# One decoder layer on one core: later w_ada loads, alternating half-array matmuls, and gathers, scores and gate loads in other places

## The chip, the cores and the metric

The kernel runs on one core of a Trainium2 chip. The time is what the device takes for one execution, in microseconds (us), and the value that counts is the median of the runs. A comparison of two such kernels can tell a difference of about 0.5% from no difference.

## What is computed

One decoder layer, 512 tokens of width 1024. Cut to what matters here:

```
mod = silu(c) @ w_ada + b_ada            # 6 vectors of 1024: sh1 sc1 gt1 sh2 sc2 gt2
h   = LN(x) * (1 + sc1) + sh1
z   = h @ w_in                           # q k v of two mixers, gates
ya  = differential attention, 8 heads, two softmax maps of key size 64 each, causal
ym  = chunkwise mLSTM, 4 heads, chunks of 128
y   = sigmoid(g_attn) * (ya @ w_br_attn) + sigmoid(g_ml) * (ym @ w_br_mlstm)
x   = LN_affine(ALPHA * x + gt1 * (y @ w_out))
h   = LN(x) * (1 + sc2) + sh2
q   = h @ peer_wq                        # 8 heads, two halves of 64 each
s   = q . sub_keys                       # 128 scores per half; top 16 of each,
                                         # then top 16 of their sums: 128 experts per token
out = sum over the 128 experts of softmax * gelu(h . u[e]) * v[e]
x   = LN_affine(ALPHA * x + gt2 * out)
```

## The kernel before

All matrix products run in split precision: an operand is a float16 high part and a float16 rest, and a product is three matmuls (high·high, high·rest, rest·high; `mm3_one`). The split costs one ScalarE and one VectorE instruction per piece (`split`, L168 and L169). Every weight piece is 128x1024 float32, goes through one of three `raw` buffers (L173) and ends in one of eight `w2` buffers.

The order of TensorE's instructions is the order in which the program is written: `Ordered` links each matmul to the one before. A scheduler places the instructions of the other engines and of the DMA queues; `P.before(r)` tells it to place r behind the last matmul written so far. That link is an order in the schedule and carries no semaphore. A queue works strictly in its order: SyncE issues nearly all loads, ScalarE the stores, GpSimd (POOL) the gathers, and an instruction that waits holds up those behind it. A `Filler` hands out TensorE work (a group of matmuls at a time) between the steps of attention, mLSTM and routing.

The stages, in us of the profiled span:

- To 84: layer norm, the first two w_ada vectors, the first projections.
- 84 to 330, attention. 32 steps of (head, query block): `at_s` (L436) computes two score maps m = 0 and 1. Map m takes rows 64m to 64m+63 of q and k, so each of its matmuls uses half of the array's rows: three matmuls of n columns (n = 128, 256, 384, 512 for the four query blocks) and one 128-row matmul that adds the causal mask (`negm`, `identb`). Before, map 0 is written whole, then map 1. Beside it `presplit` loads pieces of the tables q and u into `pre`, splits them and stores them to DRAM (`us`).
- 330 to 412, the mLSTM's last heads (`ml_s`, `ml_v`, `ml_y`; decay tiles `E`, L644 to L661).
- 412 to 570, the merge: 8 steps j, each with up to four groups of 24 matmuls. In each step `mod_col` (L306) is called for gt1, sc2, sh2 and gt2: it loads one 128x1024 block of w_ada into a `raw` buffer (tile `wad`, L311) and reduces it with one VectorE instruction (L312). These 32 blocks are the last 32 of 48. Nothing but a free buffer holds their loads back.
- 570 to 640: output projection, layer norm, h2. `gate_row` turns a column vector into a broadcast row with 8 transposes; the row h2r of token tile 0 is stored to DRAM (`h2d`).
- 640 to 1030, routing. `route(t)` for the token tiles t = 1 to 3 (t = 0 runs before): `scores` (L925) computes 4 heads of one half (12 matmuls of 64 rows), `top16` (L917 to L921) picks; then one-hot products build the dense gate matrix, staged in `gstage` and stored to DRAM (`gd`). TensorE's filler work here is the first 72 of 128 blocks of `u` (`u_pair`), whose results go to DRAM (`actd`). Tile 0 is done sparsely: `fetch` (L865) gathers a row of u per token, `dots` (L873) multiplies it with h2r. `some(dotg, n)` hands out dots: one after each of the four banks of a route, one in each of its nine one-hot steps.
- 1030 to 1060, change-over: buffers of the front part are released, h2r and gt2's row (`g2r`) are made ready, the first gate blocks (`gblk`, L1259) are loaded from `gd`.
- 1060 to 1465: `u_round(n)` and `v_round` alternate. A u round computes 4 blocks of u; a v round multiplies 4 blocks of gated activations with v: 4 times 18 matmuls. `some(sp, rate)` hands out gathers of tile 0: 7.2 in a u round, 4 in a v round (`SP_V` = 1.0 per block).
- 1465 to 1779, the held rounds: 18 v rounds without u rounds; activations (`at`) come back from `actd` (L1251), gates from `gd`; `gate` multiplies them (L1283) and splits the product. 4 gathers per round, each summed into `accg` (L1235).
- 1779 to the end: the last v round tile by tile (`last_part`), `finish` for each of the four token tiles (layer norm, store).

Of the kernel before, what the change touches and what calls it, by code (L numbers as in the profile page):

```python
# [22 lines left out]
NT = 4  # L23
# [7 lines left out]
S_ACT = 16.0  # L31
# [30 lines left out]
SP_0 = 0  # L62
SP_V = 1.0
OGN = [3, 3, 7, 7]
# [42 lines left out]
def body(tc, x, c, w_ada, b_ada, wz, wif, b_if, conv_w, conv_b, lam, subg, mlg,  # L107
# [6 lines left out]
    with pool(name="cst", bufs=1) as cst, pool(name="wts", bufs=1) as wts, \  # L114
# [21 lines left out]
        def ps_s():  # L136
            return psp.tile([128, 512], F32, name="s", tag="s", bufs=3)
# [169 lines left out]
        def mod_col(m, j, w=None):  # L307
            raw_, o, k, plus = m
            if w is None:
                w = wts.tile([128, 1024], F32, name="wad", tag="raw", bufs=3)  # L310
            nc.sync.dma_start(w, w_ada[8 * k + j])  # L311
            V.scalar_tensor_tensor(w, w, 0.5, silc, op0=ALU.mult, op1=ALU.mult,  # L312
                                   accum_out=raw_[:, j:j + 1])
            V.scalar_tensor_tensor(o[:, j:j + 1], raw_[:, j:j + 1], plus,
                                   badac[:, 8 * k + j:8 * k + j + 1], op0=ALU.add, op1=ALU.add)
# [21 lines left out]

        h2d = dr.tile([128, 1024], F32, name="h2d")
        with pool(name="fr", bufs=1) as fr:
# [106 lines left out]
            def at_s(h, i):  # L446
                n = 128 * (i + 1)
                qs = slice(i * 128, n)
                q, k = Q[h], K[h]
                if i == 0:  # L450
                    st_[h, "sums"] = wk.tile([128, 2, 4], F32, name="sums", tag="sums", bufs=3)
                sums = st_[h, "sums"]
                nm = small("nm", 4)
                Pm = []
                sms = []
                for m in range(2):
                    r = slice(64 * m, 64 * m + 64)
                    sm = ps_s()
                    sms.append(sm)
                    P.matmul(sm[:, :n], q[r, 0, qs], k[r, 0, :n], start=True, stop=False)  # L460
                    P.matmul(sm[:, :n], q[r, 0, qs], k[r, 1, :n], start=False, stop=False)
                    P.matmul(sm[:, :n], q[r, 1, qs], k[r, 0, :n], start=False, stop=False)
                    P.matmul(sm[:, qs], identb, negm, start=False, stop=True)
                    V.tensor_reduce(nm[:, m:m + 1], sm[:, :n], axis=AX.X, op=ALU.max, negate=True)
                V.tensor_scalar(nm[:, 2:4], nm[:, 0:2], 0.125 / 256.0, None, op0=ALU.mult)
                for m in range(2):
                    pm = t2("pm")
                    A.activation(pm[:, :n], sms[m][:, :n], AF.Exp, scale=0.125 / 256.0,
                                 bias=nm[:, 2 + m:3 + m], accum_out=sums[:, 1 - m, i:i + 1])
# [419 lines left out]
        with pool(name="rt", bufs=1) as rt:  # L889
# [34 lines left out]

            def scores(t, hq, p):  # L925
                ts = slice(t * 128, (t + 1) * 128)
                r = slice(64 * p, 64 * p + 64)
                ps = ps_s()
                for k in range(4):
                    h = 4 * hq + k  # L930
                    mm3(ps[:, k * 128:(k + 1) * 128], [(qT[r, h, 0, ts], qT[r, h, 1, ts],
                                                       kT[r, 0], kT[r, 1])])
                sb = t2("sb", (128, 4, 128))
                A.activation(sb, ps.rearrange("p (a b) -> p a b", a=4), AF.Copy,
                             scale=1.0 / (S_ACT * S_ACT))
                SB[t, hq, p] = sb

            banks = [(hq, p) for hq in range(2) for p in range(2)]

            def route(t):  # L940
                sv = rtile("sv", [128, 16, 16])
                si = rtile("si", [128, 16, 16], U32)
                for n, (hq, p) in enumerate(banks):
                    if (t, hq, p) not in SB:
                        scores(t, hq, p)
                    if n < 3:
                        scores(t, *banks[n + 1])
                    sb = SB[t, hq, p]
                    for k in range(4):
                        w_ = rtile("tw", [128, 128])  # L950
                        e = 8 * hq + 2 * k + p
                        top16(sv[:, e], si[:, e], sb[:, k], w_)
                        yield FILL_S / 4
                    if t > 0:
                        some(dotg, DOT_S)
# [12 lines left out]
                for h in range(8):  # L968
                    cw_ = rtile("cw_", [128, 80])
                    top16(cv[:, h], ci[:, h], cd[:, h], cw_)  # L970
                    yield FILL_S / 4
                gk = rtile("gk", [128, 8, 16])
                V.tensor_sub(gk, cv, cv[:, :, 0:1].to_broadcast([128, 8, 16]))
# [19 lines left out]
                for m in range(2):  # L993
# [10 lines left out]
                    yield FILL_S  # L1004
                if 0 < t and t + 1 < NT:
                    scores(t + 1, 0, 0)
                if t == 0:
# [153 lines left out]
            V.tensor_add(h2r, h2r, shr)  # L1161
            nc.scalar.dma_start(h2d, h2r)
            F.add("h2", weave(h2_part(1, 3), out3, H2_1))
# [21 lines left out]
        rows = big([128, 4, 1024], F32, "rows2")  # L1185
        g2r, lg, lb, h2r = [rows[:, k] for k in range(4)]
        nc.sync.dma_start(h2r, h2d)
        gate_row(gt2, g2r)
        with pool(name="vp", bufs=1) as vp:
# [4 lines left out]
            order = list(range(N1 // 4, 32)) + list(range(N1 // 4))  # L1194
            AT, WT, GB = {}, {}, {}

# [72 lines left out]

            def u_round(n, rate=SP_U - SP_V):  # L1270
                at = new_at(n)
                for i in range(4):
                    for _ in u_gen(4 * order[n] + i, at[:, i]):
                        pass
                    if n == 0:
                        G.tensor_copy(gat[0:1, i, 0:1], at[0:1, i, 0:1])
                    some(sp, rate)

            def gate(n):
# [4 lines left out]
                                op=ALU.mult)  # L1284
                w = vp.tile([128, 2, 4, TD], F16, name="w", tag="w", bufs=2)
                split(w[:, 0], w[:, 1], at, S_WT)
                WT[n] = w

# [19 lines left out]
            def v_round(n, keep_ops=None):  # L1308
                w = WT.pop(n)
                for i in range(4):  # L1310
# [5 lines left out]
                    out_part(op, BANKS, n == 0 and i == 0, False)  # L1316
                    some(sp, SP_V)
                    if i == 1 and n + 1 < len(order):
# [14 lines left out]
            ops = []  # L1333
            for k in range(6):
                gate_load(k // 4 * 2, k % 4)
            u_round(0, SP_0)
            gate(0)
            for n in range(len(order)):
# [70 lines left out]
```

## Time and profile before

| what | value |
|---|---|
| median of 3 runs | 1806.31 us (1806.1 to 1812.16) |
| profiled execution | 1810.87 us, of which the span is 1808.8 us |
| busy TensorE (PE) | 1704.3 us, 94% of the span |
| busy VectorE (DVE) | 1423.5 us, 79% |
| busy ScalarE (ACT) | 813.1 us, 45% |
| busy GpSimd (POOL) | 452.6 us, 25% |
| mean DMA rate | 268 GB/s |
| chain of work that ended last | PE 58%, DVE 16%, DMA 9%, issue 8%, POOL 4%, ACT 3% |

The profile is of one execution. A row of a wait names the instruction that waited and the one whose end released it. A row of the timeline has start, length, engine, line, operation, tiles and count; matmuls are pipelined, so a row's length runs a little into the next row, and the distance between starts is what an instruction costs.

### The profile page before, as it was taken

Reading aid. Unit: us, or ns where it says so; the run is one execution under the profiler, and the core shown is the slowest. Engines: PE = TensorE matmul, PEld = TensorE weight load, DVE = VectorE, ACT = ScalarE, POOL = GpSimd, SP = SyncE. Lnnn points to the kernel's source line nnn. Section 1 sums busy time; section 2 is a strip of 40 time slices with the busy share of each in tenths; the row PEclk is TensorE's granted clock in tenths of the full one; section 3 lists DMA queues with packets and bytes.
Section 4 is the critical chain, followed back from the end, with each engine's and each line's share of the span. In section 5 each row is a group of like instructions: output and inputs, shape, how many; then the busy total and the mean of one; then the engine's idle time right before and its main releaser. Section 6 shows DMA issues by size and latency. Waiting matters only on the chain.

```text
span 1808.8 us, 26501 instructions
## 1 busy us (share of the span) xinstructions
PE 1704.3 (94%) x9937; PEld 915.9 (51%) x9937; DVE 1423.5 (79%) x2702; ACT 813.1 (45%) x1279; POOL 452.6 (25%) x296
## 2 busy tenths in 40 slices
PE   5999999989999989999998899999999998988996
PEld 2444455445444666766655555555555543433443
DVE  7787877697666798969989658888878777577796
ACT  4556666564343433636737543333333333232332
POOL 0000000000000100110210135554556445345551
PEclk9999999989999999999999999999999999999999
DMA  8554754347776536895976999999999999988982
GB/s 337 170 191 168 248 195 142 105 157 273 273 277 231 210 114 222 285 306 193 305 258 222 334 347 357 389 349 343 341 376 331 333 336 321 342 287 320 331 325 80
DMA packets 223104, 484.89 MB, mean 268 GB/s; under 512 B 16000, under 2 KB 114560, under 8 KB 222976
## 3 DMA queue, kind: packets, MB, share of 16 engines
q1 hardware_dynamic: 124912, 286.06, 46.0%
q0 software_dynamic: 36864, 134.23, 20.2%
q10 hardware_dynamic: 61200, 62.92, 10.1%
q8 instruction: 77, 1.26, 0.3%
q14 instruction: 51, 0.42, 0.1%
HBM read 418.14 MB, written 65.01 MB: 267 GB/s over the span
## 4 chain that ended last, share of the span: by engine, by line
PE 58%; DVE 16%; DMA 9%; issue 8%; POOL 4%; ACT 3%; ACTq 1%; SPq 0%; DVEq 0%; POOLq 0%
PE mm L101 32%; PE s L101 15%; PE tr L101 6%; POOL gat L865 3%; PE o L101 3%; DVE w L169 2%; DMA gat<-in_v_dram,ev 2%; DMA gd<-gstage 1%; PE tr L104 1%; DMA vraw<-in_v_dram 1%; DMA raw<-in_u_dram 1%; DVE accg L1235 1%; DVE gat L873 1%; ACTq L914 1%; DMA at<-actd 1%
## 5 line engine op out<-in xcount | busy, mean ns | idle before, releaser
L101 PEld LDWEIGHTS <-w 128*128 128x128 f16 x7176 | 690.5, 99 | 669.3 <-issue 30.1
L101 PE MATMUL mm<-h2T,w 128*128 128x384 f16 (+2 forms) x3288 | 558.0, 327 | 12.0 <-ACT ast L857 7.4
L101 PE MATMUL s<-w,w 128*128 128x512 f16 x1152 | 275.4, 384 | 25.7 <-DVE w L169 25.7
L865 POOL DMA_INDIRECT gat<-in_v_dram,ev x128 | 240.3, 1878 | 227.6 <-DVE accg L1235 210.9
L865 POOL DMA_INDIRECT gat<-in_urows_dram,eu x128 | 179.5, 1403 | 447.6 <-DVE gat L873 352.0
L169 DVE SCALAR_TENSOR_TENSOR w<-raw,w 128x1024 f16<-128x1024 f32 x180 | 218.8, 1219 | 73.6 <-ACT w L168 73.1
L168 ACT ACTIVATE w<-vraw 128x1024 f16<-128x1024 f32 x128 | 134.9, 1055 | 284.2 <-DMA vraw<-in_v_dram 158.4
L168 ACT ACTIVATE w<-raw 128x1024 f16<-128x1024 f32 x180 | 188.2, 1053 | 85.6 <-DMA raw<-in_u_dram 34.1
L101 PE MATMUL mm<-h1T,w 128*128 128x512 f16 x960 | 219.0, 379 | 1.8 <-DVE cva L624 1.8
L101 PE MATMUL tr<-w,w 128*128 128x512 f16 x768 | 187.0, 380 | 0.0
L169 DVE SCALAR_TENSOR_TENSOR w<-vraw,w 128x1024 f16<-128x1024 f32 x128 | 155.2, 1217 | 20.2 <-ACT w L168 20.0
L1235 DVE SCALAR_TENSOR_TENSOR accg<-gat,wg,accg 128x1024 f32<-128x1024 f32 x127 | 162.3, 1278 | 10.1 <-DMA gat<-in_v_dram,ev 9.5
L1283 DVE TENSOR_TENSOR at<-at,gblk 128x1536 f32<-128x1536 f32 x32 | 56.2, 1755 | 81.1 <-DMA at<-actd 70.7
L873 DVE SCALAR_TENSOR_TENSOR gat<-gat,rows 128x1024 f32<-128x1024 f32 x89 | 107.9, 1220 | 12.5 <-DMA gat<-in_urows_dram,eu 12.4
L101 PE MATMUL mm<-w,h1T 128*128 128x512 f16 x456 | 107.7, 382 | 3.6 <-ACT h1T L168 1.8
L101 PE MATMUL o<-w,w 128*128 128x512 f16 x384 | 105.4, 385 | 0.0
L101 PEld LDWEIGHTS <-h1T 128*128 128x128 f16 x672 | 58.3, 98 | 66.0 <-issue 2.5
L165 POOL TENSOR_TENSOR ss<-ss,mhalf 128x4 f32<-128x4 f32 x8 | 8.1, 1017 | 314.7 <-DVE ss L510 284.2
L857 ACT ACTIVATE at<-mm 128x384 f32<-128x384 f32 x56 | 27.4, 489 | 129.8 <-PE mm L101 126.3
L1050 ACT ACTIVATE gstage<-tr 128x512 f32<-128x512 f32 x96 | 56.5, 598 | 55.3 <-PE tr L101 37.9
L169 DVE SCALAR_TENSOR_TENSOR pre<-pre 128x1024 f16<-128x1024 f32 x44 | 53.8, 1222 | 31.4 <-ACT pre L168 30.6
L101 PEld LDWEIGHTS <-onehot 128*128 128x128 f16 x768 | 64.0, 148 | 19.6 <-issue 9.5
(460 smaller groups left out, 1837.0 us busy)
## 6 DMA issues: line engine op xcount, KB each, us to landing
vraw<-in_v_dram SPq DMA_DIRECT2D x128, 512.0 KB, 7.5
raw<-in_u_dram SPq DMA_DIRECT2D x92, 512.0 KB, 6.5
raw<-in_wz_dram SPq DMA_DIRECT2D x64, 512.0 KB, 4.3
w<-us SPq DMA_DIRECT2D x52, 512.0 KB, 4.5
wad<-in_w_ada_dram SPq DMA_DIRECT2D x48, 512.0 KB, 5.1
gd<-gstage ACTq DMA_DIRECT2D x24, 1024.0 KB, 9.3
gblk<-gd SPq DMA_DIRECT2D x64, 384.0 KB, 9.9
us<-pre ACTq DMA_DIRECT2D x44, 512.0 KB, 4.1
```

The costliest lines, as they stand in the source:

```text
L101: self._link(self.tc.nc.tensor.matmul(*a, **k))
L104: self._link(self.tc.nc.tensor.transpose(*a, **k))
L165: G.tensor_tensor(o, i, mhalf[:, :i.shape[1]], op=ALU.pow)
L168: A.activation(hi, src, AF.Copy, scale=scale)
L169: V.scalar_tensor_tensor(lo, src, scale, hi, op0=ALU.mult, op1=ALU.subtract)
L857: A.activation(dst, ps[:, :TD], AF.Gelu, scale=RU)
L865: P.before(G.indirect_dma_start(out=g_, out_offset=None, in_=table, in_offset=bass.IndirectOffsetOnAxis(ap=e[:, k:k + 1], axis=0)))
L873: V.scalar_tensor_tensor(g_, g_, 1.0, ring["h2r"], op0=ALU.mult, op1=ALU.mult, accum_out=wg[:, k:k + 1])
L914: nc.scalar.dma_start(actd[k], a.rearrange("p a b -> p (a b)"))
L1050: A.activation(st[:, :, 4 * q4:4 * q4 + 4], ps.rearrange("p t i -> p i t"), AF.Copy, scale=1.0 / S_G)
L1235: V.scalar_tensor_tensor(accg, g_, wg[:, k:k + 1], accg, op0=ALU.mult, op1=ALU.add)
L1283: V.tensor_tensor(av, av, GB[q_ // 2][:, :, e].rearrange("p g e t -> p e g t"), op=ALU.mult)
```

## The change

1. `mod_col`: a w_ada load into a `raw` buffer is placed behind the last matmul written before it, so the 32 loads of the merge are placed behind TensorE's work up to that merge step.
2. `at_s` and `scores`: the matmuls of the two row halves alternate; in `at_s` the two masks follow together; `scores` makes both halves of four heads in one call.
3. `route`: all four banks of the next tile's scores are written at the end of a route (before: one bank, and only for t > 0); in t > 0 four more dots are handed out between the final top-16 picks.
4. gt2's row is made earlier, beside sc2 and sh2, and stored with h2r; one load brings both back.
5. The first gate loads come behind the u round 0 loads, and the first `w` buffer of the v rounds is allocated early.
6. `SP_V` for the held rounds is 0.68 instead of 1.0; in u rounds and earlier v rounds the rates stay.

```diff
-SP_V = 1.0
+SP_V = 0.68
...
         def mod_col(m, j, w=None):
             raw_, o, k, plus = m
-            if w is None:
+            lazy = w is None
+            if lazy:
                 w = wts.tile([128, 1024], F32, name="wad", tag="raw", bufs=3)
-            nc.sync.dma_start(w, w_ada[8 * k + j])
+            late = nc.sync.dma_start(w, w_ada[8 * k + j])
+            if lazy:
+                P.before(late)
...
-                sms = []
-                for m in range(2):
-                    r = slice(64 * m, 64 * m + 64)
-                    sm = ps_s()
-                    sms.append(sm)
-                    P.matmul(sm[:, :n], q[r, 0, qs], k[r, 0, :n], start=True, stop=False)
-                    P.matmul(sm[:, :n], q[r, 0, qs], k[r, 1, :n], start=False, stop=False)
-                    P.matmul(sm[:, :n], q[r, 1, qs], k[r, 0, :n], start=False, stop=False)
+                sms = [ps_s(), ps_s()]
+                for a, b in ((0, 0), (0, 1), (1, 0)):
+                    for m in range(2):
+                        r = slice(64 * m, 64 * m + 64)
+                        P.matmul(sms[m][:, :n], q[r, a, qs], k[r, b, :n],
+                                 start=a + b == 0, stop=False)
+                for sm in sms:
                     P.matmul(sm[:, qs], identb, negm, start=False, stop=True)
+                for m, sm in enumerate(sms):
                     V.tensor_reduce(nm[:, m:m + 1], sm[:, :n], axis=AX.X, op=ALU.max, negate=True)
...
-            def scores(t, hq, p):
+            def scores(t, hq):
                 ts = slice(t * 128, (t + 1) * 128)
-                r = slice(64 * p, 64 * p + 64)
-                ps = ps_s()
+                pss = [ps_s(), ps_s()]
                 for k in range(4):
                     h = 4 * hq + k
-                    mm3(ps[:, k * 128:(k + 1) * 128], [(qT[r, h, 0, ts], qT[r, h, 1, ts],
-                                                       kT[r, 0], kT[r, 1])])
+                    for a, b in ((0, 0), (0, 1), (1, 0)):
+                        for p in range(2):
+                            r = slice(64 * p, 64 * p + 64)
+                            P.matmul(pss[p][:, k * 128:(k + 1) * 128], qT[r, h, a, ts], kT[r, b],
+                                     start=a + b == 0, stop=a == 1)
...
                     if (t, hq, p) not in SB:
-                        scores(t, hq, p)
-                    if n < 3:
-                        scores(t, *banks[n + 1])
+                        scores(t, hq)
+                    if n == 1 and (t, 1, 0) not in SB:
+                        scores(t, 1)
...
                     top16(cv[:, h], ci[:, h], cd[:, h], cw_)
                     yield FILL_S / 4
+                    if t > 0 and h % 2 == 1:
+                        some(dotg, DOT_S)
...
-                if 0 < t and t + 1 < NT:
-                    scores(t + 1, 0, 0)
+                if t == 0:
+                    F.need("q_all")
+                if t + 1 < NT:
+                    scores(t + 1, 0)
+                    scores(t + 1, 1)
...
-            nc.scalar.dma_start(h2d, h2r)
+            nc.scalar.dma_start(h2d[:, 0], h2r)
+            g2s = t4("g2s")
+            gate_row(gt2, g2s)
+            nc.scalar.dma_start(h2d[:, 1], g2s)
...
-        nc.sync.dma_start(h2r, h2d)
-        gate_row(gt2, g2r)
...
+                    if n == 0 and i == 3:
+                        for k in range(4):
+                            gate_load(0, k)
+                        nc.sync.dma_start(rows[:, 0:2], h2d)
...
-                    some(sp, SP_V)
+                    some(sp, SP_V if n >= NF else 1.0)
...
-            for k in range(6):
-                gate_load(k // 4 * 2, k % 4)
             u_round(0, SP_0)
+            for k in range(2):
+                gate_load(2, k)
             gate(0)
```

`NF` is 14, the number of the first held round.

Where the instructions stand now. First TensorE in attention, at the first step; `s_803` and `s_809` (before), `s_803` and `s_804` (changed) are the score maps of the two row halves, `identb` and `negm` the mask. Before:

```order
L101 LDWEIGHTS q_624
L101 MATMUL s_803<-k_657,q_624 128x128
L101 LDWEIGHTS q_624
L101 MATMUL s_803<-k_657,q_624 128x128
L101 LDWEIGHTS q_624
L101 MATMUL s_803<-k_657,q_624 128x128
L101 LDWEIGHTS identb_82
L101 MATMUL s_803<-negm_88,identb_82 128x128
L101 LDWEIGHTS q_624
L101 MATMUL s_809<-k_657,q_624 128x128
```

Changed:

```order
L101 LDWEIGHTS q_624
L101 MATMUL s_803<-k_657,q_624 128x128
L101 LDWEIGHTS q_624
L101 MATMUL s_804<-k_657,q_624 128x128
L101 LDWEIGHTS q_624
L101 MATMUL s_803<-k_657,q_624 128x128
L101 LDWEIGHTS q_624
L101 MATMUL s_804<-k_657,q_624 128x128
```

Map 0 and map 1 now take turns, and the mask no longer stands between them.

Second the queue of SyncE between attention and merge; `wba` and `wbm` are the branch weights, `wz` gate weights, `xt` a tile of x for the output projection, `pre` a piece of u for `presplit`. Before:

```order
L173 DMA raw<-in_wba_dram 128x1024
L311 DMA wad<-in_w_ada_dram 128x1024 x4
L173 DMA raw<-in_wbm_dram 128x1024
L311 DMA wad<-in_w_ada_dram 128x1024 x4
L173 DMA raw<-in_wz_dram 128x1024
L173 DMA raw<-in_wbm_dram 128x1024
L311 DMA wad<-in_w_ada_dram 128x1024 x4
```

Changed:

```order
L173 DMA raw<-in_wba_dram 128x1024
L1083 DMA xt_5437<-in_x_dram 128x1024
L312 DMA wad<-in_w_ada_dram 128x1024 x4
L195 DMA pre<-in_u_dram 128x1024 x2
L173 DMA raw<-in_wbm_dram 128x1024
L312 DMA wad<-in_w_ada_dram 128x1024 x4
L195 DMA pre<-in_u_dram 128x1024 x2
L173 DMA raw<-in_wz_dram 128x1024
L173 DMA raw<-in_wbm_dram 128x1024
```

The first four w_ada loads now stand behind the load of `xt`, whose buffer is free when TensorE has transposed head 0 of the mLSTM, and two `pre` loads, whose buffer is free when TensorE is done with the mLSTM's last scores, stand ahead of the first `wbm`.

Third VectorE at the end, from the last split of a v block on; `accg` sums the gathered rows of token tile 0, `fo` is the output of the other tiles. Before:

```order
L169 SCALAR_TENSOR_TENSOR w_16293<-vraw,w_16293 128x1024
L1235 SCALAR_TENSOR_TENSOR accg<-gat,wg,accg 128x1024 x4
L1330 SCALAR_TENSOR_TENSOR fo<-s,rows_10955 128x512
L1235 SCALAR_TENSOR_TENSOR accg<-gat,wg,accg 128x1024
L1202 TENSOR_TENSOR fo<-fo,ax_5393 128x512
L1238 TENSOR_TENSOR accg<-accg,rows_10955 128x512 x2
```

Changed (the last three of 13 sums of `accg`, and what follows them):

```order
L1249 SCALAR_TENSOR_TENSOR accg<-gat,wg,accg 128x1024
L1348 SCALAR_TENSOR_TENSOR fo<-tr,rows_10995 128x512
L1249 SCALAR_TENSOR_TENSOR accg<-gat,wg,accg 128x1024
L1216 TENSOR_TENSOR fo<-fo,ax_5393 128x512
L1249 SCALAR_TENSOR_TENSOR accg<-gat,wg,accg 128x1024
L1218 BN_STATS bst<-fo 128x6
L1252 TENSOR_TENSOR accg<-accg,rows_10995 128x512 x2
L1216 TENSOR_TENSOR accg<-accg,ax_5393 128x512 x2
L1348 SCALAR_TENSOR_TENSOR fo<-tr,rows_10995 128x512
```

Thirteen sums stand behind the last split instead of five, and tile 0's finish stands among that of the last tile instead of ahead of the second.

## Rows read from the trace of the kernel before

**Rows 1.** Stretches: length, busy PE, PEld, DVE, ACT, POOL (count), PEclk, DMA share, GB/s.

```profile
84.00:330.00 246.00, 238.89 (x1385) 120.01 (x1383) 192.30 (x439) 154.51 (x361) 7.13 (x7) 1.00 0.52 181
330.00:412.00 82.00, 74.00 (x404) 40.78 (x402) 64.15 (x150) 50.72 (x155) 4.03 (x4) 0.94 0.47 150
412.00:570.00 158.00, 157.80 (x737) 72.22 (x736) 103.41 (x152) 63.91 (x80) 3.47 (x2) 1.00 0.78 278
640.00:1020.00 380.00, 362.82 (x2781) 241.41 (x2781) 343.53 (x1075) 201.60 (x280) 46.94 (x38) 0.99 0.76 247
1020.00:1060.00 40.00, 32.41 (x209) 20.66 (x208) 13.23 (x15) 15.70 (x24) 1.40 (x4) 0.87 1.02 334
1060.00:1465.00 405.00, 405.00 (x2186) 213.75 (x2185) 339.42 (x370) 151.57 (x179) 221.95 (x147) 1.00 0.97 352
1465.00:1779.00 314.00, 288.26 (x1295) 127.86 (x1294) 228.79 (x180) 97.73 (x87) 151.63 (x73) 0.97 0.88 313
1779.00:1809.00 30.00, 15.92 (x74) 7.06 (x72) 23.61 (x43) 7.18 (x12) 3.46 (x4) 0.85 0.19 70
```

**Rows 2.** Waits of all engines, 1430 to the end: us in total, times, longest.

```profile
DVE at L1283 <- DMA at<-actd: 70.7, 10, 11.3
...
PE s L101 <- DVE w L169: 25.7, 7, 5.4
```

**Rows 3.** Timeline of TensorE, the last wait in a held round.

```profile
1700.25 2.40 PE L101 MATMUL s<-w,w 128*128 128x512 f16 x7 [3.68 <-DVE w L169]
```

**Rows 4.** Groups of TensorE, attention's half-array matmuls: busy us, mean ns, idle before.

```profile
L101 PE MATMUL s<-k,q 64*128 64x128 f16 (+3 forms) x192 | 37.0, 299 | 2.2 <-ACT pm L468 2.2
```

**Rows 5.** Timeline of TensorE, one attention step with 512 columns.

```profile
103.84 0.82 PE L101 MATMUL s<-k,q 64*128 64x512 f16 x3
104.60 0.23 PE L101 MATMUL s<-negm,identb 128*128 128x128 bf16 x1
104.76 0.82 PE L101 MATMUL s<-k,q 64*128 64x512 f16 x3
105.57 0.59 PE L101 MATMUL mm<-h1T,w 128*128 128x512 f16 x2
```

**Rows 6.** Timeline of TensorE, scores: two banks in a row, one bank alone.

```profile
673.65 1.31 PE L101 MATMUL s<-kT,qT 64*128 64x128 f16 x24
...
680.85 0.84 PE L101 MATMUL s<-kT,qT 64*128 64x128 f16 x12
```

**Rows 7.** Waits of VectorE, 640 to 1020.

```profile
DVE sv L917 <- ACT sb L934: 18.2, 4, 7.8
```

**Rows 8.** Tile wad, 330 to 412: ns min/median/max, first and last start.

```profile
L312 DVE SCALAR_TENSOR_TENSOR wad<-wad,silc x13: 1212/1219/1246, 351.1 to 405.4; 128x1024 f32<-128x1024 f32 x13
```

**Rows 9.** Waits of TensorE, 330 to 412.

```profile
PE s L101 <- DVE E L661: 6.1, 3, 3.0
```

**Rows 10.** Timeline at the change-over, SyncE's queue and ScalarE.

```profile
1024.86 4.69 SPq L1259 DMA_DIRECT2D gblk<-gd  x3
...
1039.30 1.06 ACT L168 ACTIVATE w<-raw 128x1024 f16<-128x1024 f32 x1 [5.42 <-DMA raw<-in_u_dram]
```

**Rows 11.** DMA issues, 1465 to 1779: KB each, median us from issue to landing.

```profile
vraw<-in_v_dram SPq DMA_DIRECT2D x67, 512.0 KB, 7.0
at<-actd SPq DMA_DIRECT2D x32, 384.0 KB, 6.1
gblk<-gd SPq DMA_DIRECT2D x26, 384.0 KB, 10.0
gat<-in_v_dram,ev POOLq DMA_INDIRECT x73, 8.3
```

**Rows 12.** Timeline of GpSimd, a gather late in the kernel.

```profile
1749.76 1.68 POOL L865 DMA_INDIRECT gat<-in_v_dram,ev  x1 [0.65 <-DVE accg L1235]
```

**Rows 13.** Timeline of VectorE, the last two half-tile operations.

```profile
1804.40 1.41 DVE L1221 SCALAR_TENSOR_TENSOR fo<-fo,rs,rows 128x512 f32<-128x512 f32 x2
```

**Rows 14.** DMA issues, 412 to 570.

```profile
wad<-in_w_ada_dram SPq DMA_DIRECT2D x17, 512.0 KB, 5.2
```

More of the change, by code (lines that the diff above doesn't have):

```diff
@@ L336, in gate_row @@
                 A.activation(r[:, hf * 512:(hf + 1) * 512], ps.rearrange("p a b -> p (a b)"), AF.Copy)
-        h2d = dr.tile([128, 1024], F32, name="h2d")
+        h2d = dr.tile([128, 2, 1024], F32, name="h2d")
         with pool(name="fr", bufs=1) as fr:
@@ L923, in body @@
             SB = {}
-            def scores(t, hq, p):
+            def scores(t, hq):
                 ts = slice(t * 128, (t + 1) * 128)
-                r = slice(64 * p, 64 * p + 64)
-                ps = ps_s()
+                pss = [ps_s(), ps_s()]
                 for k in range(4):
                     h = 4 * hq + k
-                    mm3(ps[:, k * 128:(k + 1) * 128], [(qT[r, h, 0, ts], qT[r, h, 1, ts],
-                                                       kT[r, 0], kT[r, 1])])
[L933 to L936, printed above, removed]
+                    for a, b in ((0, 0), (0, 1), (1, 0)):
[3 more added lines that the diff above has]
+                                     start=a + b == 0, stop=a == 1)
+                for p, ps in enumerate(pss):
+                    sb = t2("sb", (128, 4, 128))
+                    A.activation(sb, ps.rearrange("p (a b) -> p a b", a=4), AF.Copy,
+                                 scale=1.0 / (S_ACT * S_ACT))
+                    SB[t, hq, p] = sb
             banks = [(hq, p) for hq in range(2) for p in range(2)]
@@ L1185, in body @@
         rows = big([128, 4, 1024], F32, "rows2")
-        g2r, lg, lb, h2r = [rows[:, k] for k in range(4)]
-        nc.sync.dma_start(h2r, h2d)
-        gate_row(gt2, g2r)
+        h2r, g2r, lg, lb = [rows[:, k] for k in range(4)]
         with pool(name="vp", bufs=1) as vp:
@@ L1194, in body @@
             order = list(range(N1 // 4, 32)) + list(range(N1 // 4))
-            AT, WT, GB = {}, {}, {}
+            NF = 32 - N1 // 4
+            AT, GB = {}, {}
+            WT = {0: vp.tile([128, 2, 4, TD], F16, name="w", tag="w", bufs=2)}
             def finish(t, o, halves):
@@ L1268, in ahead, with u_round @@
                     gate_load(n + 2, 2 + i // 2)
-            def u_round(n, rate=SP_U - SP_V):
+            def u_round(n, rate=SP_U - 1.0):
                 at = new_at(n)
@@ L1284, in gate @@
                                 op=ALU.mult)
-                w = vp.tile([128, 2, 4, TD], F16, name="w", tag="w", bufs=2)
-                split(w[:, 0], w[:, 1], at, S_WT)
-                WT[n] = w
+                if n not in WT:
+                    WT[n] = vp.tile([128, 2, 4, TD], F16, name="w", tag="w", bufs=2)
+                split(WT[n][:, 0], WT[n][:, 1], at, S_WT)
             ACC = [[ps_s(), ps_s()], [ps_s(), ps_o()],
```

## The prediction

> **What bounds the kernel now.** I read the stretches first [rows 1], then the waits and the timeline inside the stretches where TensorE isn't full. TensorE works without a gap from 1060 to 1465 (405.00 of 405) and from 412 to 570; there only fewer or cheaper matmuls could help. It falls short in four places: 8.0 us from 330 to 412, 17.2 from 640 to 1020, 7.6 from 1020 to 1060, 25.7 from 1465 to 1779. [...]
>
> In the held rounds (1465 to 1779) the reader is to see a chain: VectorE's gate product waits for `at` (70.7 us in 10 waits), and TensorE for the split behind it (25.7 us, 7 waits) [rows 2]. DMA moves 352 GB/s at a share of 0.97 from 1060 to 1465 [rows 1]; I take that as what it can do with this mix. A held round with gate loads wants, per 15.5 us (279.7 us of full work over 18 rounds, from 314 less 25.7 and 9.4): 4 v blocks and 4 gathers of 524 KB, two `at` and 26/14 `gblk` loads of 393 KB [rows 11], 5.7 MB or 367 GB/s. That is more than 352. The last rounds have no gate loads: 5.0 MB, 321 GB/s, and after 1700.25 TensorE waits no more [rows 3].
>
> **The change part by part.** The sum is made against the profiled execution, 1810.87 us; the median of the runs shown is 4.56 us lower.
>
> *Attention, alternating halves.* The half-array matmuls are busy 37.0 us [rows 4], 192 of them in 64 triples. In a step with 512 columns a triple costs 0.76 (103.84 to 104.60), the first mask 0.16, the second half 0.81 with its mask [rows 5]. A triple costs 0.06 less than its busy time, so all 64 cost 33 and half of them 16.6. If the two halves run beside each other, 16.6 go; a mask that stands behind another saves the 0.10 that the change of shape costs, 3.2 over 32 steps. Together 19.8. Whether they run beside each other is to be seen in the scores, where two halves meet once: 12 matmuls take 0.84, 24 take 1.31, so the second twelve add 0.47 instead of the 0.67 that twelve cost alone (0.84 less a drain of 0.17) [rows 6]. About 30% of it was hidden, with only one border between the halves. Ends: 5 us (30% of 16.6, no saving at the masks) and 20. TensorE is 97% busy there and VectorE 78% [rows 1], so little else takes the place; I take 16, as every neighbour is now of the other half, but VectorE (192.3 us in what would be 230) will cost a few short waits. [...]
>
> *Routing.* 16 banks of 12 score matmuls at 0.67 become 8 pairs: about 5 us less TensorE work. VectorE's waits for scores, 18.2 us [rows 7], lose their cause when the scores are made a route ahead. Against that stand 12 more dots at 1.22 (an instruction of the shape and length of the `wad` reduction [rows 8]) plus gathers that are waited for, 15 to 20 us of VectorE in a stretch where it is busy 343.5 of 380. A pair of scores needs two of three banks, so the second pair waits for a ScalarE copy, 1 us in each of three routes. Net -4; ends -16 (TensorE's idle time goes) and +12 (the dots lie bare).
>
> *w_ada loads.* 13 reductions, 15.9 us of VectorE, stand among the mLSTM's last heads [rows 8], where TensorE waits 6.1 for `E` [rows 9]. They move into the merge, where VectorE has 54 us free and DMA 0.78 [rows 1]. That saves up to 8 of waits and 4.9 of clock. But in SyncE's queue the first `wbm` now stands behind the `xt` load, four w_ada loads and two `pre` loads that wait for TensorE, and TensorE enters the merge with fewer weights ready. I give half back: -6; ends -12 and +6.
>
> *Change-over.* The `gblk` loads wait in SyncE's queue for the gate stores (4.69 us of queue at 1024.86) and u loads stand behind them; ScalarE then waits 5.42 for u [rows 10]. With six u loads of the next rounds ahead of the gates this goes, as do gt2's transposes. TensorE misses 7.6 us and 5.2 of clock here. What stays is the wait for the `gd` stores. gt2's row costs 1.5 us at its new place. Net -9; ends -14 and -3.
>
> *Held rounds.* 0.68 times 4 gathers per round make 5.0 MB, 324 GB/s, as much as the rounds that ran without a wait (321). Missing are 25.7 us and 9.4 of clock, together 35. I take 31; ends -35 and -10.
>
> *Tail.* 77 + 128 gathers are left for the rounds. u rounds 1 to 13 take 93.6, 14 v rounds 56, 17 held rounds 46.2: 195.8, so 9 come into the last part. Behind the last split stand 13 sums, four gathers of them on their way. The others come one in 2.33 us (1.68 and 0.65) [rows 12], 21 us, and about as long as TensorE needs to its end (12 us from the last split to the last part, then 15.9 [rows 1]). Then eight half-tile operations of tile 0 at 0.70 [rows 13] come behind TensorE's end: +6; ends 0 and +14 (a landing of 8.3 us [rows 11] bare).
>
> Sum: -16 -4 -6 -9 -31 +6 = **-60**, 1810.9 - 60 = 1751 for a profiled execution, 1746 as a median; rounded to **1747**. All ends together: -97 and +14, medians of 1709 and 1820.
>
> **The rivals.**
>
> *Order, not bytes, holds the held rounds.* Four `gblk` loads land after 10.0 us each [rows 11] ahead of `at` in the same queue; with fewer gathers they may still be late. For it: DMA's share is 0.88 on the mean of the stretch [rows 1], not 0.97. Against it: the rounds without gate loads. Then that term is -10 and the time 1767. [...]
>
> *Routing gains all of TensorE's idle time.* Term -16, time 1734. For it 18.2 us of waits; against it VectorE's load.
>
> *Attention is held by its softmax chain.* Term -5, time 1757. For it: ScalarE and VectorE are in a chain over three steps; against it: only 7 us of 246 are lost now.
>
> *The w_ada loads do not move the work.* The link has no semaphore; four loads still stand ahead of each `wbm`. Term 0, time 1752.
>
> *Slower: the merge becomes bound by the three `raw` buffers.* A step needs 4 w_ada blocks and 4 weights, each holding a buffer for its landing and 1.2 (w_ada) or 2.3 us (split). At a landing of 5.2 [rows 14] that is (4·6.4 + 4·7.5)/3 = 18.5 us; TensorE's step, 96 matmuls at 158/737, is 20.6. It decides from a landing of 6 us on; at 10, as `gblk` has it, a step takes 31, +74 over seven steps, and the whole comes out at +14: 1820. For it: now all eight steps carry their w_ada loads, DMA is at 278 GB/s already and half a step is not loaded ahead. Against it: the later steps carry the same loads today, and TensorE is full in them.
>
> **How the numbers follow.** Forecast 0.57, order 0.15, routing 0.12, attention 0.09, w_ada without effect 0.04, slower 0.03. The range leaves out the far corner of the ends and the slow rival: 1716 to 1784. A measurement tells 0.5% (9 us) from no change; faster than 1797 are all cases but the slow one and a pile of upper ends: faster 0.95, same 0.02, slower 0.03.
>
> **What would show it.** Right: alternating half-array triples at about half their busy time (20 instead of 37 us), no `E` waits beside `wad`, no ScalarE wait for u at the change-over, waits for `at` under 15 us, a tail of some 36 us from the last part's start. Wrong: waits for `raw` weights in the merge, 20 us or more of waits for `at`, or VectorE at 100% with TensorE waiting in routing.

## The result, and the profile after

The changed kernel takes **1947.86 us** in the median of 4 runs (1944.98 to 1949.39); the kernel before took 1806.20 in runs beside it. The ratio is 1.077, 95% interval 1.075 to 1.079: slower by some 140 us, against a forecast of 1747 us and a range up to 1784. The profiled execution took 1949.39 us, its span is 1947.3.

Where the time went is read by cutting each span at the same events: the end of the last k,q matmul, the last VectorE half of the `ymT` split and of the `yT` split, the first scores, the last copy into `gstage`, the first gate product, TensorE's last matmul. Every piece holds the same stage in all kernels, whatever the clock time. Three kernels from the experiments below stand beside the two:

| stage, us | before | changed | e1 | e8 | e14 |
|---|---|---|---|---|---|
| to the last k,q matmul | 317.1 | 311.8 | 312.1 | 316.3 | 319.1 |
| to the last ymT | 106.9 | 103.4 | 106.9 | 109.0 | 104.6 |
| merge, to the last yT | 144.5 | **280.8** | 144.5 | 144.6 | 144.6 |
| to the first scores | 50.8 | 54.7 | 53.6 | 51.4 | 51.4 |
| routing, to the last gstage | 421.5 | 434.0 | 432.6 | 424.7 | 419.8 |
| change-over, to the first product | 22.5 | 19.9 | 19.1 | 22.4 | 22.7 |
| rounds, to TensorE's end | 731.6 | 716.4 | 724.2 | 711.4 | 698.5 |
| behind TensorE's end | 13.9 | 26.3 | 26.5 | 47.9 | 13.8 |
| span | 1808.8 | 1947.3 | 1819.5 | 1827.7 | 1774.5 |

136.3 of the 138.5 us lie in the merge. The other stages add up to +2.2, where the forecast had -54 for them. So there are two things to explain. Each column is one profile: routing spreads from 419.8 to 424.7 over the seven kernels that leave it as before, so a few us in one stage say little by themselves.

The merge of the changed kernel, as a stretch (columns as in [rows 1]):

```profile
415.00:696.00 281.00, 167.06 (x679) 68.64 (x677) 124.97 (x179) 64.92 (x72) 2.47 (x1) 0.78 0.51 187
```

[Rows 1] had this merge with TensorE busy 157.80 of 158 us at a clock of 1.00 and 278 GB/s. Now TensorE stands still for 114 us of 281, and every engine and DMA is idle more than before. The mean granted clock is 0.78, and the 312 matmuls on `h1T` took 441 ns each in the mean, against 379 at a clock of 1.00 in the merge before; TensorE's busy time exceeds 144.5 by 22.6 us. That is no resource in short supply; it is a chain. The waits of the same stretch, TensorE's, VectorE's, and those of SyncE's queue from 412 to 700 (us, times, longest):

```profile
PE mm L101 <- ACT w L168: 99.1, 7, 15.0
PE s L101 <- ACT w L168: 13.0, 1, 13.0
...
DVE gg L731 <- PE s L101: 98.6, 13, 11.6
...
SPq L312 <- DVE mcgt L317: 159.9, 10, 29.5
```

TensorE waits 8 times, some 14 us each, for a split weight; VectorE waits for TensorE's merge sums; SyncE's w_ada load waits for VectorE's w_ada work. One such round, in the timeline of SyncE's queue:

```profile
421.30 20.14 SPq L312 DMA_DIRECT2D wad<-in_w_ada_dram  x4
...
442.48 0.38 SPq L173 DMA_DIRECT2D raw<-in_wz_dram  x1
```

VectorE at the same time:

```profile
437.13 0.69 DVE L731 SCALAR_TENSOR_TENSOR gg<-gg,s 128x512 f32<-128x512 f32 x1 [6.21 <-PE s L101]
...
439.24 0.69 DVE L169 SCALAR_TENSOR_TENSOR yT<-gg,yT 128x512 f16<-128x512 f32 x1 [0.69 <-ACT yT L168]
439.85 1.22 DVE L315 SCALAR_TENSOR_TENSOR wad<-wad,silc 128x1024 f32<-128x1024 f32 x1
...
441.19 1.22 DVE L315 SCALAR_TENSOR_TENSOR wad<-wad,silc 128x1024 f32<-128x1024 f32 x1
```

ScalarE, then TensorE:

```profile
449.99 2.00 ACT L168 ACTIVATE w<-raw 128x1024 f16<-128x1024 f32 x2 [1.66 <-DVE pre L169]
```

```profile
436.28 0.81 PE L101 MATMUL s<-ymT,w 128*128 128x512 f16 x3
451.10 1.03 PE L101 MATMUL mm<-h1T,w 128*128 128x512 f16 x2 [14.01 <-ACT w L168]
```

Read them in order of time. Three w_ada blocks fill the three `raw` buffers (a ring: w_ada blocks and weights take them in turn); their loads were issued by 431, and the last had landed by 434.4. TensorE ends its merge step at 437.09. Only then can VectorE do `gg` and `yT`, and only behind these, in its order, stand the w_ada reductions, from 439.85. Each frees a buffer; the first goes to the step's fourth block, the second to the `wz` weight (issued 442.48), which lands 6 us later, is split from 449.99 (behind a 1.66 us wait of ScalarE for a `pre` split), and TensorE goes on at 451.10. The next step's weights can't be fetched while TensorE works, since the buffers hold blocks whose reader stands behind that work.

### The profile page after: what moved, and what is told of

Read it like the earlier page. It is cut to its first block, busy times and chain, and to the rows that moved or that the text cites. A ratio compares the mean times of both kernels' runs of the same rounds, so it can differ in the third digit from the quotient of the medians.

```text
span 1947.3 us, 26496 instructions
## 1 busy us (share of the span) xinstructions
PE 1705.7 (88%) x9937; PEld 907.7 (47%) x9937; DVE 1426.4 (73%) x2702; ACT 812.8 (42%) x1279; POOL 444.2 (23%) x296
## 4 chain that ended last, share of the span: by engine, by line
PE 32%; DVE 24%; issue 14%; DMA 14%; POOL 10%; ACT 5%; SPq 1%; ACTq 0%; POOLq 0%; DVEq 0%
PE mm L101 19%; POOL gat L868 9%; PE s L101 8%; DVE w L169 4%; DMA at<-actd 3%; PE tr L101 3%; DMA pre<-in_u_dram 2%; DMA gat<-in_urows_dram,eu 2%; DVE gat L876 2%; DMA raw<-in_wz_dram 1%; DVE pre L169 1%; DMA raw<-in_u_dram 1%; PE o L101 1%; DVE accg L1249 1%; ACT w L168 1%
## 5 line engine op out<-in xcount | busy, mean ns | idle before, releaser
L101 PE MATMUL mm<-h1T,w 128*128 128x512 f16 x960 | 239.9, 403 | 106.0 <-ACT w L168 99.1
L868 POOL DMA_INDIRECT gat<-in_v_dram,ev x128 | 224.0, 1750 | 276.3 <-DVE accg L1249 267.4
L868 POOL DMA_INDIRECT gat<-in_urows_dram,eu x128 | 187.1, 1461 | 435.5 <-DVE gat L876 302.6
L876 DVE SCALAR_TENSOR_TENSOR gat<-gat,rows 128x1024 f32<-128x1024 f32 x77 | 93.6, 1220 | 26.4 <-DMA gat<-in_urows_dram,eu 26.2
L101 PE MATMUL o<-w,w 128*128 128x512 f16 x384 | 103.3, 379 | 0.0
L731 DVE SCALAR_TENSOR_TENSOR gg<-gg,s 128x512 f32<-128x512 f32 x16 | 11.0, 685 | 98.6 <-PE s L101 98.6
L876 DVE SCALAR_TENSOR_TENSOR gat<-gat,h2rr 128x1024 f32<-128x1024 f32 x51 | 62.0, 1217 | 25.4 <-DMA gat<-in_urows_dram,eu 25.4
L168 ACT ACTIVATE pre<-pre 128x1024 f16<-128x1024 f32 x44 | 46.3, 1053 | 75.1 <-DMA pre<-in_u_dram 71.7
```

The costliest lines, as they stand in the source:

```text
L101: self._link(self.tc.nc.tensor.matmul(*a, **k))
L168: A.activation(hi, src, AF.Copy, scale=scale)
L731: V.scalar_tensor_tensor(g_, g_, 1.0, ps, op0=ALU.add, op1=ALU.mult)
L868: P.before(G.indirect_dma_start(out=g_, out_offset=None, in_=table, in_offset=bass.IndirectOffsetOnAxis(ap=e[:, k:k + 1], axis=0)))
L876: V.scalar_tensor_tensor(g_, g_, 1.0, ring["h2r"], op0=ALU.mult, op1=ALU.mult, accum_out=wg[:, k:k + 1])
```

## The experiments

All ratios are to the kernel before, measured beside.

**What makes the merge slow: e1 to e4.** e1 takes the order out of the changed kernel, e2 puts it alone into the kernel before; e3 and e4 keep it and change the buffers or the place:

```
e1  -            if lazy:
    -                P.before(late)
e2  +            if lazy:
    +                P.before(late)
e3  -  w = wts.tile([128, 1024], F32, name="wad", tag="raw", bufs=3)
    +  w = t4("wad")
e4  -                P.before(late)
    +                P.before(late, pins[j])   # last matmul ahead of step j - 1
```

> The changed kernel without the order of the lazy w_ada loads behind TensorE; all else of the change stays. Theory (the order alone makes the loss): the merge, 280.8 us in the changed kernel from the last ymT split to the last yT split, goes back to 144.5, as before, and about 1947.9 - 136 = 1812 us is left; the other stages of the changed kernel add up to only +2 against the kernel before, so there is no more to win (1800 to 1815). Rival (the other stages of the changed kernel are slow because the merge is late and its clock low): the forecast without its w_ada term, 1753 us.

Measured: 1816.73 us, ratio 1.003 (1.001 to 1.004); the merge 144.5 us. The theory holds, 2 us above its range: the order makes the whole loss of the merge, and the other stages still win nothing together (+10.7 against before in the profile). So the rest of the change wins nothing even without it.

> The kernel before with that order alone: every w_ada load of the merge behind the last matmul issued so far. Theory: the merge takes 270 to 290 us instead of 144.5, the whole 1925 to 1950. Rival (it needs the other edits, the new place of the x tile's load among them): within 20 us of 1806.

Measured: 1942.29 us, ratio 1.073 (1.070 to 1.075); the merge 278.8 us. The order alone does it.

> The changed kernel, order kept, but the w_ada blocks lie in the four t4 buffers, which stand free in the merge, instead of the three raw buffers through which the merge weights pass. Theory A (the ring of raw buffers: a step's weights get their buffers only behind that step's w_ada blocks, and these only behind the step before on TensorE and VectorE): the merge falls to 145 to 165 us, the whole to 1800 to 1835. Theory B (VectorE's and SyncE's order hold it, whatever buffers there are): 1900 or more.

Measured: 1812.13 us, ratio 1.002 (1.001 to 1.004). Theory A holds. The merge with the same late blocks in other buffers:

```profile
415.00:559.00 144.00, 144.00 (x669) 65.29 (x668) 111.16 (x171) 56.40 (x65) 2.46 (x1) 1.00 0.90 346
```

TensorE is full at 346 GB/s, with the 32 blocks loaded in the merge (the first three issued up to 1.4 us ahead of it). So bytes are not the cause, and late loads by themselves cost the merge nothing: it takes the order together with the shared ring. SyncE's queue changed with the buffers, though: behind the last k,q matmul, twelve weight loads stand ahead of the next w_ada load in e3, two in the changed kernel. So e3 does not part the ring from the queue that goes with it. In the round shown above the ring suffices: all three buffers hold w_ada blocks until 441, and no weight could be loaded until one came free.

> The changed kernel with each step's w_ada loads held behind the last matmul before the step before, one merge step earlier than in the change; buffers as in the change. Theory A: a step's blocks are out of the ring before TensorE ends the step before, so its weights can be loaded ahead: the merge 145 to 170 us, the whole 1800 to 1840. Theory C (eight loads a step through three buffers are too many, as in the forecast's slow rival: 18.5 us a step at a landing of 5.2, 31 at 10): the merge stays above 220 us, the whole above 1885.

Measured: 1837.43 us, ratio 1.016 (1.012 to 1.021); the merge 167.8 us. Theory A again, though at its upper end: one step of lead gives back 113 of 136 us through the same three buffers. TensorE waits there for long once, 12.15 us at 435.86; behind it the merge runs full:

```profile
451.00:580.00 129.00, 128.32 (x595) 57.99 (x593) 90.27 (x125) 51.59 (x60) 2.47 (x1) 1.00 0.84 306
```

So eight loads a step are not too many for three buffers.

**What the other terms were worth: e5 to e8.** e5, e6 are e1 with one more edit, e7, e8 the kernel before with one part of the change:

```
e5  AT_B = 4;  accg = h2r
e6  -                    if t > 0 and h % 2 == 1:
    -                        some(dotg, DOT_S)
e7  the diff's part in at_s
e8  SP_V = 0.68 in the held rounds; u_round's rate unchanged
```

> As e1_no_order, with four `at` buffers instead of three (accg takes the place of h2r, whose last reader is done by then, to make room). Theory R (a ring, not bytes: each `at` load waits for the split three products back, which stands one product ahead of its own): VectorE's waits for `at` from 1465 on fall from 71.6 to under 20 us, TensorE's for the split from 13.2 to under 3, and the whole is 8 to 20 us shorter than e1_no_order. Theory B (bytes: DMA can't bring v, at, gblk and gathers in time): the waits stay above 50 us and the whole within 5 us of e1_no_order.

Measured: 1830.30 us, ratio 1.011 (1.009 to 1.013). VectorE waits 79.8 us for `at`, TensorE 21.9. Theory R falls, and the kernel is slower than e1, so B, which expected no change, isn't shown either. The trace suggests why. In e1 a gate product and its split stood 38 us apart (`at` of the product at 1558.3 is split at 1596.5); with four buffers it is 60 (1590.6 and 1651.0). The extra buffer let VectorE's order put the product yet another round ahead. That this is what made e5 slower was not tried by itself (`accg` moved too); it gave the theory of e9.

> As e1_no_order, without the twelve more dot products in the routes. Theory (the dots lie bare on VectorE and wait for gathers, as the upper end of the forecast's routing term had it): from the first scores to the last gstage 432.6 us falls to 417 to 425; the gathers come later instead, so the whole gains 0 to 10. Rival (the scores made a whole route ahead, or their wait for PSUM, are what costs): that stretch stays above 430.

Measured: 1823.44 us, ratio 1.007 (1.005 to 1.009). Routing falls to 420.4 us, as expected. The whole does not gain: its median is 6.7 us above that of e1. 16 of the 128 sums now come after TensorE's end (4 in e1), and that piece is 46.9 us, 20.4 longer. But the two profiles don't show the loss, their spans are 1815.9 us (e6) and 1819.5 (e1), so where the 6.7 us lie stays open. VectorE's waits for gathers while routing in e1:

```profile
DVE gat L874 <- DMA gat<-in_urows_dram,eu: 25.4, 10, 5.7
```

The same wait in e6, and before:

```profile
DVE gat L874 <- DMA gat<-in_urows_dram,eu: 13.7, 4, 5.2
...
DVE gat L873 <- DMA gat<-in_urows_dram,eu: 4.8, 1, 4.8
```

The scores themselves did what was forecast: their group was busy 13.0 us before and is 6.9 in e6.

> The kernel before with the alternating halves in the attention alone. Theory (TensorE's work falls by 15 us, but the softmax chain and the two PSUM banks that must be free at once take 10 back): 3 to 8 us faster than before. Rival (the forecast's term): 16 faster.

Measured: 1803.85 us, ratio 0.998 (0.996 to 0.9995). The theory holds, barely outside no change. The stretch from 84 to the last ymT, before:

```profile
84.00:424.00 340.00, 324.69 (x1846) 166.79 (x1844) 267.22 (x614) 210.62 (x526) 12.16 (x12) 0.98 0.51 172
```

In e7, and below it TensorE's waits there:

```profile
84.00:419.00 335.00, 309.65 (x1846) 159.58 (x1843) 265.11 (x614) 210.91 (x526) 12.92 (x12) 0.98 0.51 175
```

```profile
PE s L101 <- ACT pm L468: 8.8, 5, 3.7
...
PE mm L101 <- DVE cva L624: 5.3, 4, 2.8
```

15.0 us less work, 5.0 us less time; idle grew from 15.3 to 25.4. Most of the new waits are for `pm`, the exponential that frees an `s` bank (2.2 us before, [rows 4]): there are three such banks, and a pair wants two at once.

> The kernel before with 0.68 instead of 1.0 gathers a block in the held rounds alone. Theory (the ring of `at` buffers holds those rounds, bytes only in part; what isn't gathered there is summed up at the end): the stretch from the first to the last gate product 6 to 14 us shorter, the tail behind it 8 to 14 longer, the whole within 6 us of before. Rival (the forecast): 25 us faster, -31 and +6.

Measured: 1824.12 us, ratio 1.007 (1.005 to 1.010). The rounds up to TensorE's end are 20.2 us shorter (711.4), the piece behind it 34.0 longer. My own expectation missed the size of both, and the whole (13 us slower, not within 6). The two pieces of the tail, from the last gate product:

```profile
1720.90:1779.80 58.90, 58.90 (x273) 26.52 (x271) 41.66 (x37) 11.20 (x10) 21.95 (x16) 1.00 0.57 198
1779.80:1827.70 47.90, 0.00 (x1) 0.00 (x0) 38.07 (x51) 7.17 (x12) 18.72 (x17) 0.55 0.58 200
```

In the first GpSimd issues 16 gathers, one in 3.7 us; 16 sums are left when TensorE ends, where before there was none.

**Bytes or order: e9 to e12, e14.** The edit, `held` in the gate function:

```
-                V.tensor_tensor(av, av, ...)
+                product = V.tensor_tensor(av, av, ...)
+                if held(n):
+                    P.before(product)
```

> As e1_no_order, with each held round's gate product ordered on VectorE behind the last TensorE matmul issued before it. Theory G (neither bytes nor the count of buffers: VectorE's order has each gate product two rounds ahead of its split, 38 us in e1_no_order, so an `at` buffer stands idle between the two, its next load comes one product ahead of its own, and the whole queue of VectorE stands at the product): the product and its split are under 8 us apart, VectorE's waits for `at` from 1465 on fall from 71.6 to under 15 us, TensorE's from 13.2 to under 3, and the whole is 10 to 20 us shorter than e1_no_order. Theory B (bytes): the waits move from the gate product to the v blocks, TensorE waits 10 us or more, the whole is within 5 us of e1_no_order.

Measured: 1800.64 us, ratio 0.996 (0.994 to 0.997), 16 us under e1. No wait for `at` is left, and TensorE waits 0.7 us for a split.

> The kernel before with the alternating halves in the attention and the ordered gate products, all gathers where they were (1.0 a block). Theory G: the held rounds' 25.7 us of waits and the clock behind them go without any gather moved: 20 to 32 us faster than e7_attention_alone, 1772 to 1785. Theory B, which was the forecast's reason (5.7 MB a held round are more than DMA brings): at most 10 us faster than e7_attention_alone.

Measured: 1774.30 us, ratio 0.980 (0.978 to 0.982). Theory G.

> The kernel before with the ordered gate products alone, all its gathers in place. Theory G: VectorE's waits for `at` from 1465 on fall from 66 to under 5 us, TensorE's from 25.7 to under 3, the tail stays within 5 us of its 72.6, the whole is 24 to 32 us faster than before (e10 was 29.5 faster than the kernel with the attention edit alone). Theory B (bytes): the waits stay or move to the v blocks, less than 10 us faster.

Measured: 1778.33 us, ratio 0.983 (0.979 to 0.986): 31 us faster than before with one added dependency and every gather in its place. The tail counted from the last product shrank to 38.3, since that product now comes later; from TensorE's end it is 13.8 us as before. VectorE before, from the product at 1546.35, whose `at` is split at 1588.64:

```profile
1546.35 1.76 DVE L1283 TENSOR_TENSOR at<-at,gblk 128x1536 f32<-128x1536 f32 x1 [10.07 <-DMA at<-actd]
1548.03 1.22 DVE L169 SCALAR_TENSOR_TENSOR w<-vraw,w 128x1024 f16<-128x1024 f32 x1
```

VectorE in e14, a product and its split:

```profile
1566.06 1.75 DVE L1283 TENSOR_TENSOR at<-at,gblk 128x1536 f32<-128x1536 f32 x1
1567.73 1.22 DVE L169 SCALAR_TENSOR_TENSOR w<-vraw,w 128x1024 f16<-128x1024 f32 x1
1568.87 1.28 DVE L1235 SCALAR_TENSOR_TENSOR accg<-gat,wg,accg 128x1024 f32<-128x1024 f32 x1
1570.06 1.75 DVE L169 SCALAR_TENSOR_TENSOR w<-at,w 128x1536 f16<-128x1536 f32 x1
```

The product before came 42 us ahead of need and stood 10.07 us for its `at`, with the v splits that TensorE did need behind it. In e14 it comes 4 us ahead and waits for nothing. The held stretch of e14:

```profile
1465.00:1735.00 270.00, 268.51 (x1245) 121.54 (x1243) 222.37 (x174) 96.86 (x85) 111.53 (x70) 1.00 0.96 356
```

> The changed kernel without the order of the w_ada loads, without the twelve more dots and with 1.0 gathers a block, plus the ordered gate products: scores ahead, gates behind the u loads and the rows from DRAM stay. Theory: these are worth 0 to 8 us over e10_att_gate_order (5 us less TensorE work in the scores, a shorter change-over). Rival (a pair of scores and the change-over cost as much as they save): within 3 us of e10_att_gate_order or slower.

Measured: 1772.18 us, ratio 0.979 (0.977 to 0.981), 2 us under e10. That lies in the range of the theory and of the rival, so it decides nothing: scores ahead and gates behind u loads win nothing that shows.

> As e10_att_gate_order, with FILL_B 2500 instead of 2300: each attention step gets 0.4 us more of other matmuls as cover for its softmax chain, about what the alternating halves took from it. Theory (the chain's latency, not an engine's load, ate ten of the attention's fifteen us): TensorE's idle time to the last k,q matmul falls by 5 to 10 us and the whole by 3 to 8 against e10_att_gate_order. Rival (VectorE's and ScalarE's load is the bound, or the mLSTM's heads lack the cover then): within 3 us or slower.

Measured: 1773.75 us, ratio 0.981 (0.979 to 0.982): the rival. TensorE's waits for `pm` fell from 9.8 in e10 to 4.4 us, those for `cva` rose from 4.2 to 9.6. Cover moves the waits; what would remove them stays open.

**The idea of loading late, with buffers of its own: e13, e15.** Both are e11 with the changed kernel's order and e3's buffers, e15 with `FILL_B` 2500 as well.

> As e11_all_but_two, but with the changed kernel's order of the w_ada loads and the blocks in the four t4 buffers. Theory (late loads cost nothing once the weights' ring is free of them, and spare VectorE in the mLSTM's last heads): the stretch from the last k,q matmul to the last ymT 103 to 106 us against 108 in e11, the merge 144 to 147, the whole 2 to 8 us faster than e11. Rival (nothing is won: TensorE waits there for E, which other VectorE work holds): within 2 us of e11.

Measured: **1770.34 us**, ratio 0.979 (0.975 to 0.982), the shortest median of all, but not to be told from e11: the whole is within the rival's 2 us. From the last k,q matmul to the last ymT (the mLSTM's last heads) it takes 103.3 us, e11 108.1: the heads do gain, as the theory had it.

> As e13_late_own_buffers with FILL_B 2500: both effects side by side. If the late loads free VectorE in the mLSTM heads, the filler taken from there is missed less: 1 to 5 us faster than e13. If the heads lack cover: slower than e13 by 1 to 4.

Measured: 1775.52 us, ratio 0.981 (0.977 to 0.984). Slower than e13 by 5, but not for the reason given: the heads take 102.8 us, the attention 6 more. Inconclusive.

## Why the prediction was wrong

**w_ada loads (-6): it cost 136.** This is the step that failed. It counted the reductions and looked at SyncE's queue, and took back half for a first step with fewer weights ready. It never asked where the *readers* of the blocks would stand in VectorE's order. A load tied behind TensorE's last step puts its reduction behind that step's `gg` and `yT`; as blocks and weights share one ring of three, the weights then wait a whole step. The slow rival, at 0.03, named the ring and the wait ("waits for `raw` weights in the merge"), but priced it by landings and let it decide from 6 us on. Landings were 4.9 us for w_ada and 4.6 for `wz` over the whole changed kernel:

```profile
raw<-in_wz_dram SPq DMA_DIRECT2D x64, 512.0 KB, 4.6
...
wad<-in_w_ada_dram SPq DMA_DIRECT2D x48, 512.0 KB, 4.9
```

By its own rule it would not have come to pass. Its argument against, that the later steps carry the same loads today, was true of the bytes and not of the order. VectorE before, in the merge, has a reduction ahead of a `gg` and a split:

```profile
440.54 1.22 DVE L312 SCALAR_TENSOR_TENSOR wad<-wad,silc 128x1024 f32<-128x1024 f32 x1
...
441.87 0.68 DVE L728 SCALAR_TENSOR_TENSOR gg<-gg,s 128x512 f32<-128x512 f32 x1
442.47 1.22 DVE L169 SCALAR_TENSOR_TENSOR w<-raw,w 128x1024 f16<-128x1024 f32 x1
```

The gain in the heads is real (4.8 us, e13 against e11): from the last k,q matmul to the last ymT the six kernels with held-back loads take 101.4 to 103.4 us, the ten others with `FILL_B` 2300 104.6 to 109.0 (e12, with 2500, 103.8).

**Held rounds (-31): -7.4 in e1, -20.2 alone (e8).** The premise failed: that 352 GB/s is "what it can do with this mix", so that 5.7 MB a round were too much. e14 moves them all at 356 GB/s and TensorE waits 1.5 us. 352 kept TensorE full from 1060 to 1465 [rows 1], and was no ceiling; the trace of before had slices above it, up to 401, in its own held stretch (GB/s in 40 slices of 1465 to 1735):

```profile
GB/s 367 401 279 389 295 381 354 154 337 381 361 388 177 323 388 361 382 183 305 333 372 372 318 149 331 323 368 394 186 319 340 368 378 269 218 329 393 398 334 362
```

Slices near 400 beside slices near 150 look like a chain that starts and stops. The same stretch of e14, where the waits are gone, doesn't fall under 257 ahead of its last two slices:

```profile
GB/s 408 409 272 384 337 391 409 405 370 344 411 403 397 292 380 408 408 325 336 405 408 401 292 364 410 406 330 331 395 407 403 286 312 404 407 409 268 257 81 158
```

The 35 us that the forecast saw in these rounds were there: from the first product to TensorE's end e14 wins 33.1, 24.2 of waits and 8.9 of busy time. The rival "Order, not bytes" was right on the kind of cause; it blamed `gblk` in SyncE's queue, and it was VectorE's own order: in e14 four `gblk` loads still stand right ahead of two `at` loads in that queue. No run shows by itself the time that the forecast's sums call "of clock" (4.9, 5.2 and 9.4 us); it was the author's estimate, the length of a stretch times the shortfall of its granted clock from 1.00 in [rows 1]. What the runs showed in its place: in the held rounds a clock of 1.00 in e14 (0.96 before, both from 1465 to 1735) with those 8.9 us less busy time, in the heads 4.8 us (e13 against e11) and in the change-over 3.4 (e1), waits and clock together. The rounds gained 13 us less in e1 than in e8: TensorE stands still for 18.0 us of them against 11.1, and is busy 5.9 us longer; why was not followed.

**Attention (-16): -5.0 in e7, -2.5 in e10 against e14.** In e7 TensorE's work fell by 15.0, so the pricing of the matmuls was right. In e1 a 512-column step reads

```profile
162.05 0.82 PE L101 MATMUL s<-k,q 64*128 64x512 f16 x6
```

six matmuls in the time of three [rows 5]; the group is busy 20.8 us, 37.0 in [rows 4]. In that step the second half was hidden whole (0.82 us for six, 0.82 for three). The failed clause is "a few short waits": they were 10 us. The rival held by the softmax chain (-5) had the size; the banks are the likeliest part of it, which was not tried by itself.

**Routing (-4): +11.1 in e1, -1.1 without the dots (e6).** The forecast's upper end, "the dots lie bare", came true; twelve dots cost 12 us (432.6 in e1, 420.4 in e6). With them VectorE, busy 372 of 421.5 us before, waits 11.7 us more for gathers (25.4 in e1, 13.7 in e6).

**Tail (+6): +12.6 in e1, inside its end of +14; +34.0 in e8.** The step "one in 2.33 us, and about as long as TensorE needs to its end" failed: up to TensorE's end a gather is issued in 3.7 us, in e1 as in e8. Behind it stand tile 0's finish and 4 sums in e1, 16 in e8, on a VectorE that also has tiles 1 to 3 to finish. In e8 the 20 us won in the rounds are paid back here, and 14 more.

**Change-over (-9): -3.4 in e1**, the forecast's weak end, and -2.6 in the changed kernel.

Summed up, e1 would have been -54 by the forecast and came out at +10.7 in its profiled span (+7.7 by the medians). Every gain was forecast from the stage that was relieved; what fell short was held by order (held rounds), by a chain (attention), or was work moved to a place where it lay bare (dots, gathers). Two slips in the prediction's sums move nothing: 314 less 25.7 and 9.4 is 278.9 and not 279.7, 15.5 us a round either way, and 1746 was written as 1747.

## What to carry to other kernels

When a load is delayed, ask which buffer its consumer will hold, who else takes buffers from that ring, and where in the consuming engine's order the release will stand; an order without a wait of its own can still close a circle through a shared ring (the merge at 278.8 us in e2, 144.5 before). An instruction that an engine runs long ahead of need isn't free: if it waits, all behind it wait (10.07 us at 1546.35 before), and pinning the gate product down to its time (one dependency) won 31 us where taking gathers out of the rounds (e8) won nothing in the whole. Before a mean rate is called a limit, look whether single slices exceed it.

## What was not expected of the hardware

With the gate products ordered (e14), DMA carried 356 GB/s over 270 us of held rounds, with slices up to 411, beside a TensorE that was busy 268.51 of 270 us at a granted clock of 1.00; and 346 GB/s in e3's merge. With a fourth `at` buffer e5 is slower than e1 (ratios 1.011 and 1.003), and its products stand yet further ahead of their splits (60 us against 38); that the one causes the other is not shown.
